# Counting three per cent more for a 512-column row in the planner's clock of a two-layer hybrid decoder trunk

## Chip, cores and metric

One core of one Trainium2 chip. The metric is the device time of one execution in microseconds; a kernel's time is the median of its runs. Beside the timed runs there is one profiled execution, from which every duration below is taken.

## What is computed

The reference is two layers of a decoder trunk on a sequence of 256 positions with 1024 features, in float32. Cut to what matters:

```
for i in range(2):
    h = rms_norm(x, norm_g[i])
    rq, rk, rv, rz, mq, mk, mv, mz = split(h @ w_in[i])        # 1024 -> 8 groups of 512
    r_out = silu(rz) * retention(rotary(rq), rotary(rk), rv, ret_norm_g[i])
    m_out = silu(mz) * moba(rms_norm(mq, q_norm_g[i]), rms_norm(mk, k_norm_g[i]), mv, rel_bias)
    x = x + concat([r_out, m_out]) @ w_out[i]                  # 1024 -> 1024
    gate = sigmoid(rms_norm(x) @ w_ple_gate[i])                # 1024 -> 1024
    x = x + gate * rms_norm(p[i] @ w_ple[i], ple_norm_g[i])    # 256 -> 1024
```

Retention has 4 heads of 128 with an exponential decay and a group norm per head. The block attention has 4 heads of 128; with 256 positions there is one block, so it is causal softmax attention with a relative bias.

## The kernel before

**Tiles.** The 256 positions are two row tiles (m = 0, 1) of 128. The 1024 features are 8 slices (k) of 128, so the activations lie transposed, as 128x128 stationary tiles. Weights are streamed as moving operands of 128x512. Each product of weights is made of three matmuls with split operands, high by high, high by low, low by high (`mm3`, L383, L384, L385); the parts are made by a copy on ScalarE (L336 for a weight, L635 for an activation) and a subtraction on VectorE (L339, L637). The first group of the first layer has its own routine (L531), and the per-layer embedding another (L720 to L722).

**Stages.** In each layer TensorE runs the eight input projections in the order MQ, MK, RQ, RK, MZ, MV, RV, RZ, then the output projection (first the slices k = 4 to 7, which are the attention's, then k = 0 to 3, the retention's), the embedding, and the gate projection. Each weight stage is 512 KB pieces of two slices: a load on SyncE's queue, a ScalarE copy, a VectorE subtraction. Results are turned back to transposed form by a ScalarE copy to 16-bit halves (L599), a DMA transpose on the same SyncE queue (L609) and VectorE copies (L618).

**Four groups of small matmuls** per layer are put in between the rows of the projections: `moba_scores` (L928, L910), `moba_out` (L938, which ends with the retention's own scores, L988), `ret_scores` (L910) and `ret_out` (L938). After `ret_out` comes a chain: statistics and scale of the group norm (L1009 to L1019), the normalising on ScalarE (L1026), the product with the gate RZ on VectorE (L1054, which reads the accumulator bank that RZ held, and L1059, after which the plan counts the bank as free), then turning, gain (L632) and split (L635, L637) into the stationary tiles that the output projection's slices k = 0 to 3 read. The accumulator pool `acc` has four banks, and RZ's two row tiles hold two of them while the output projection opens four accumulations.

**What sets the order.** The instruction streams of all engines are laid out at build time by the class `Flow`, a list scheduler written by hand. It keeps one clock per engine. Work that is not TensorE's is in chains (generators) whose steps have an engine and a cost in us; `pick` takes the step that can start first, and among those of one engine that can start the one with the smallest key. A chain's key is fixed when it begins (`flow.soon(slack)`: TensorE's clock then plus a slack), a weight stage's key is its due time less a lead of 5.7 to 9.6 us. TensorE's own order is the program's, and each step of it moves its clock: `flow.row(us)` first lays all other work that starts by then, and adds the us. The time that this clock shows is used in three ways:

```
ROW = 0.22
TILE = 12 * ROW
flow.row(3 * ROW * (1.0 if cols.stop - cols.start == GW else 0.53))      # in mm3, L381
return flow.clock[PE] + (i - now[0]) * TILE                               # due, L354
if any(c is None for c in cs) or not all(c.done and c.ready + margin <= flow.clock[PE] for c in cs):
    return                                                                # tick, L393
```

So ROW is the us that TensorE's clock counts for one matmul with 512 columns (L381, and L530 in the first group, L719 in the embedding), and twelve of them, TILE, are what one piece of weights is taken to last when due times are worked out. `tick` is asked after every second `mm3`, that is after six rows, and puts the next of the four groups in when all chains that it needs are finished and `margin` us have gone by on TensorE's clock (2.9, 2.0, 2.2 and 0.3 us). The small matmuls have costs of their own (0.22, 0.36), which are written as numbers, and so have all steps of the other engines. None of these numbers is an instruction: they decide only in which order each engine's instructions stand, and which of the borrowed buffers a weight piece gets. The engines then run by semaphores.

Of the kernel before, what the change touches and what calls it, by code (L numbers as in the profile page):

```python
# [50 lines left out]
EARLY = {0: FIRST, "late": S, ("K", 0): GW, 1: BLOCK, ("K", 1): GW, **{k: BLOCK for k in range(2, KT)}}  # L51

PE, ACT, DVE, POOL, SP = range(5)
ROW = 0.22
LANES, LINE = 4, 4
TILE = 12 * ROW
HOP = 0.15
# [186 lines left out]
def tile_hybrid_trunk(ctx: ExitStack, tc: tile.TileContext, early, x, pT, ple_g, rel_bias,  # L244
# [126 lines left out]
    def lanes(w):  # L371
        return w.rearrange("p (l t n) -> p t l n", t=LANES, n=LINE)

    def columns(w, sl):
        return lanes(w)[:, sl.start // P:sl.stop // P]

    def mm3(ps, a, m, k, stage, kk, start, stop, cols=slice(0, GW)):
        a.need(m, k)
        wh, wl = stage.part(kk // 2)[kk % 2]
        ah, al = a.of(m, k)  # L380
        flow.row(3 * ROW * (1.0 if cols.stop - cols.start == GW else 0.53))  # L381
        wh, wl = columns(wh, cols), columns(wl, cols)
# [129 lines left out]
    def first_rows(k, ps, start, stop, key=()):  # L512
# [9 lines left out]
        for i, (which, w, c) in enumerate(order):  # L522
# [3 lines left out]
            for j, sl in enumerate([slice(0, S), slice(S, GW)] if halves else [slice(0, GW)]):  # L526
                if j:
                    flow.need(firsts["late"])
                for m in range(MT):
                    flow.row(0.12 if halves else ROW)  # L530
                    nc.tensor.matmul(ps[m][:, sl], (a0.lo if which[0] == "lo" else a0.hi)[:, k, m * P:(m + 1) * P],  # L531
# [159 lines left out]
    def embed(l):  # L691
# [22 lines left out]
        for m in range(MT):  # L714
            ps = [bank(mix_p, "mix") for _ in range(2)]
            for n in range(2):
                for k, (wh, wl) in enumerate(w.part(n)):
                    ah, al = (v[:, k, m * P:(m + 1) * P] for v in (ph, pl))
                    flow.row(3 * ROW)  # L719
                    nc.tensor.matmul(ps[n], ah, lanes(wh), start=k == 0, stop=False)  # L720
# [564 lines left out]
```

## Time and profile before

| | |
|---|---|
| median of 3 runs | 300.57 us (299.64 to 301.93) |
| the profiled execution, device time | 301.4 us |
| its span, first to last instruction | 299.5 us |
| mean granted TensorE clock | 0.997 |
| VectorE, ScalarE, GpSimd busy | 254.7, 215.2, 31.5 us |
| DMA moved | 69.76 MB |

The profile counts busy time per engine: PE is TensorE's matmuls, PEld its loads of stationary tiles, DVE VectorE, ACT ScalarE, POOL GpSimd, SP SyncE with its DMA queue. A row of the timeline gives start, busy time, engine, line, operation and tiles, how many instructions it merges, and in brackets the idle time before it with what ended that. A row of the stages gives the stretch, its length, busy time with the number of instructions for each engine, the granted clock (PEclk), the DMA share and GB/s.

### The profile page before, as it was taken

The page shows a single profiled execution, that of the slowest core. Times are in us where ns is not written, and L with a number is a line of the kernel's source. Part 1 is how long each engine was busy: PE and PEld are TensorE (multiplying, and loading weights), DVE is VectorE, ACT ScalarE, POOL GpSimd, SP SyncE. Part 2 cuts the span into 40 slices and gives each one's busy share as a digit, 9 for nine tenths or more (in the row PEclk, how much of TensorE's full clock was granted, in tenths as well). Part 3 has the DMA queues.
Part 4 walks back from the last instruction along what each step waited for, and adds up shares of the span by engine and source line. Part 5 has one row for each costly group of instructions (what it writes and reads, how often), then busy time and mean ns, then how long its engine had stood idle before and what let it go on. Part 6 is the DMA issues. An engine that isn't in the chain of part 4 may idle for free.

```text
span 299.5 us, 4292 instructions
## 1 busy us (share of the span) xinstructions
PE 292.0 (98%) x1411; PEld 246.9 (82%) x1411; DVE 254.7 (85%) x461; ACT 215.2 (72%) x376; POOL 31.5 (11%) x44
## 2 busy tenths in 40 slices
PE   8999999999999989999999999999999999999994
PEld 4788888888899866888888888888889988888884
DVE  3968798999998999789999379999978899969932
ACT  3879966599755985998494696599764879499211
POOL 6005200000000300031003220000000030001200
PEclk9999999999999999999999999999999999999998
DMA  6999999999977858987789669857993994963011
GB/s 227 362 416 404 243 216 396 377 266 186 296 286 216 328 138 283 160 233 264 190 240 287 210 176 188 305 101 219 305 325 105 224 363 117 275 182 71 0 72 70
DMA packets 61773, 69.76 MB, mean 233 GB/s; under 512 B 46260, under 2 KB 47160, under 8 KB 61624
## 3 DMA queue, kind: packets, MB, share of 16 engines
q1 hardware_dynamic: 61712, 69.50, 77.8%
q8 instruction: 11, 0.18, 0.3%
q14 instruction: 10, 0.08, 0.1%
q0 software_dynamic: 32, 0.01, 0.0%
q10 hardware_dynamic: 8, 0.00, 0.0%
HBM read 57.42 MB, written 1.05 MB: 195 GB/s over the span
## 4 chain that ended last, share of the span: by engine, by line
PE 91%; DVE 3%; DMA 2%; ACT 1%; issue 1%; SPq 0%; DVEq 0%
PE acc L385 25%; PE acc L384 25%; PE acc L383 25%; PE acc L531 4%; PE mix L938 4%; PE mix L910 2%; DMA a<-in_early 2%; DVE wl L339 2%; PE mix L722 1%; PE mix L721 1%; PE mix L720 1%; PE mix L385 1%; PE mix L384 1%; PE mix L383 1%; PE mix L988 1%
## 5 line engine op out<-in xcount | busy, mean ns | idle before, releaser
L383 PE MATMUL acc<-wh,a 128*128 128x512 f32 (+1 forms) x292 | 110.3, 378 | 1.4 <-DVE tok L1054 1.4
L385 PE MATMUL acc<-wh,a 128*128 128x512 f32 (+1 forms) x292 | 109.9, 376 | 0.0
L384 PE MATMUL acc<-wl,a 128*128 128x512 f32 (+1 forms) x292 | 109.8, 376 | 0.0
L339 DVE TENSOR_TENSOR wl<-wst,wh 128x1024 fp32r<-128x1024 f32 x78 | 94.0, 1220 | 8.1 <-ACT wh L336 8.1
L336 ACT CAST wh<-wst 128x1024 fp32r<-128x1024 f32 x78 | 80.8, 1052 | 27.7 <-PE acc L385 18.0
L383 PEld LDWEIGHTS acc<-wh,a 128*128 128x128 f32 x292 | 54.8, 188 | 11.0 <-DVE tok L1054 1.8
L385 PEld LDWEIGHTS acc<-wh,a 128*128 128x128 f32 x292 | 54.8, 188 | 9.5
L384 PEld LDWEIGHTS acc<-wl,a 128*128 128x128 f32 x292 | 54.8, 188 | 9.2
L599 ACT COPY u<-tok 128x1024 uint16<-128x1024 uint16 x30 | 30.9, 1049 | 8.7 <-DVE tok L836 4.4
L651 POOL TENSOR_TENSOR ro<-rs_t,neghalf 128x4 f32<-128x4 f32 x4 | 5.8, 1460 | 133.2 <-DVE rs_t L649 133.2
L1160 ACT ACTIVATE tmp<-acc,hr 128x512 f32<-128x512 f32 (+1 forms) x9 | 5.8, 639 | 16.2 <-PE acc L385 16.2
L599 ACT COPY u<-x_t 128x1024 uint16<-128x1024 uint16 x12 | 12.5, 1042 | 6.3 <-DVE x_t L1116 5.1
L618 DVE COPY tmp<-w 128x512 uint16<-128x512 uint16 x40 | 15.9, 460 | 0.7 <-DMA w<-u 0.7
L635 ACT CAST a<-tmp 128x512 fp32r<-128x512 f32 x20 | 12.2, 617 | 5.7 <-DVE tmp L632 4.3
L637 DVE TENSOR_TENSOR a<-tmp,a 128x512 fp32r<-128x512 f32 x20 | 13.6, 686 | 0.5 <-ACT a L635 0.5
L618 DVE COPY T<-w 128x512 uint16<-128x512 uint16 x32 | 13.0, 464 | 1.0 <-DMA w<-u 0.9
L1163 DVE SCALAR_TENSOR_TENSOR tmp<-tmp,E 128x512 f32<-128x512 f32 (+1 forms) x9 | 5.7, 628 | 8.0 <-ACT tmp L1160 8.0
L938 PEld LDWEIGHTS mix<-V,PS 128*128 128x128 f32 x96 | 11.3, 192 | 0.3
L531 PE MATMUL acc<-wh,a 128*128 128x512 f32 (+1 forms) x42 | 11.0, 380 | 0.4 <-ACT wh L437 0.4
L938 PE MATMUL mix<-V,PS 128*128 128x128 f32 x96 | 11.4, 275 | 0.0
L383 PE MATMUL acc<-T,a 128*128 128x512 f32 x28 | 10.7, 383 | 0.0
L385 PE MATMUL acc<-T,a 128*128 128x512 f32 x28 | 10.7, 383 | 0.0
(143 smaller groups left out, 446.6 us busy)
## 6 DMA issues: line engine op xcount, KB each, us to landing
wst<-in_w_in SPq DMA_DIRECT2D x59, 512.0 KB, 6.1
wst<-in_w_out SPq DMA_DIRECT2D x16, 512.0 KB, 6.4
wst<-in_w_gate SPq DMA_DIRECT2D x16, 512.0 KB, 5.5
wst<-in_w_ple SPq DMA_DIRECT2D x4, 512.0 KB, 7.8
wst<-in_early SPq DMA_DIRECT2D x4, 384.0 KB, 7.1
a<-in_early SPq DMA_DIRECT2D x3, 384.0 KB, 5.8
x_t<-in_x SPq DMA_DIRECT2D x1, 1024.0 KB, 11.4
gb<-in_ple_g SPq DMA_DIRECT2D x2, 512.0 KB, 5.9
```

Of the source, the lines that this page charges most:

```text
L336: nc.scalar.copy(hi, s)
L339: nc.vector.tensor_tensor(lo, s, hi.bitcast(F32), op=ALU.subtract)
L383: nc.tensor.matmul(ps, ah, wh, start=start, stop=False)
L384: nc.tensor.matmul(ps, ah, wl, start=False, stop=False)
L385: nc.tensor.matmul(ps, al, wh, start=False, stop=stop)
L531: nc.tensor.matmul(ps[m][:, sl], (a0.lo if which[0] == "lo" else a0.hi)[:, k, m * P:(m + 1) * P], columns(w, sl), start=start and i + j == ...
L599: nc.scalar.copy(u, src.bitcast(U16).rearrange("p (n t) -> p t n", t=2))
L618: nc.vector.tensor_copy(v, w[:, t].rearrange("p (h b) k -> p h (b k)", h=v.shape[1]))
L635: nc.scalar.copy(h, src)
L637: nc.vector.tensor_tensor(a.lo[:, k0:k0 + 4, m * P:(m + 1) * P], src, h.bitcast(F32), op=ALU.subtract)
L910: nc.tensor.matmul(ps, w[a], x[b], start=i == 0, stop=i == 2)
L938: nc.tensor.matmul(ps[:, h * DH:(h + 1) * DH], lhs(h, m, b), v[:, b, h * DH:(h + 1) * DH], start=b == 0, stop=b == m)
```

## The change

One constant: the clock counts 0.227 us for a row in place of 0.22, and TILE with it 2.724 us in place of 2.64. No instruction is added or taken away, and no size, buffer or slack is changed.

```
-ROW = 0.22
+ROW = 0.227
 LANES, LINE = 4, 4
 TILE = 12 * ROW
```

## Prediction

> **What bounds the kernel now.** I read the page first, then TensorE's waits, then stages, then the timeline where TensorE waits. The page's engine totals:
>
> ```profile
> span 299.5 us, 4292 instructions
> PE 292.0 (98%) x1411; PEld 246.9 (82%) x1411; DVE 254.7 (85%) x461; ACT 215.2 (72%) x376; POOL 31.5 (11%) x44
> ```
>
> TensorE is busy almost throughout, VectorE is next. The list of TensorE's own waits:
>
> ```profile
> PE acc L383 <- DVE tok L1054: 1.4, 1, 1.4
> PE mix L282 <- PEq L1274: 0.8, 1, 0.8
> PE acc L531 <- ACT wh L437: 0.4, 1, 0.4
> PE acc L385 <- DVE a L637: 0.4, 1, 0.4
> PE acc L383 <- ACT a L635: 0.2, 1, 0.2
> ```
>
> The second and third are the start. The other three are one place, found by cutting the span into stages of TensorE alone (start:end, length, busy and instructions, clock, DMA share, GB/s):
>
> ```profile
> 8.64:50.58 41.94, 41.94 (x190) 1.00 0.99 335
> 50.58:84.59 34.01, 34.01 (x165) 1.00 1.06 295
> 105.68:116.44 10.76, 8.80 (x37) 1.00 0.75 212
> 116.44:191.48 75.04, 75.04 (x338) 1.00 0.82 227
> 294.80:299.50 4.70, 0.39 (x4) 0.79 0.14 49
> ```
>
> The first row has 190 matmuls back to back, 41.94 / 190 = 0.2207 us each. The fourth has 338, two of them running in from before: 75.04 / 336 = 0.2233 us. So the planner's old 0.22 was 0.3% short in one stretch and 1.5% in the other, and the new 0.227 is 2.9% and 1.7% long. The chip's rows do not move with the constant, only the order does. In the third stage 12 triples start, 36 x 0.2233 = 8.04 us of work in 10.76 us: **2.72 us are lost**, and that is all that order can still give in the middle. The last stage, 4.70 us, is the tail after the last matmul.
>
> **The place of the loss** is the first layer's output projection. TensorE there:
>
> ```profile
> 92.28 2.84 PE L938 MATMUL mix<-V,PS 128*128 128x128 f32 x24
> ...
> 100.32 0.38 PE L383 MATMUL acc<-wh,a 128*128 128x512 f32 x1
> ...
> 106.13 0.38 PE L385 MATMUL acc<-wh,a 128*128 128x512 f32 x1
> 107.92 0.49 PE L383 MATMUL acc<-wh,a 128*128 128x512 f32 x1 [1.41 <-DVE tok L1054]
> ...
> 114.11 0.48 PE L385 MATMUL acc<-V,a 128*128 128x512 f32 x1 [0.38 <-DVE a L637]
> ```
>
> and VectorE, which it waits for:
>
> ```profile
> 103.58 0.69 DVE L1054 TENSOR_TENSOR tok<-T,acc 128x512 f32<-128x512 f32 x1 [0.30 <-ACT T L1026]
> 104.30 0.69 DVE L1059 SCALAR_TENSOR_TENSOR tok<-tmp,tok 128x512 f32<-128x512 f32 x1
> 104.91 2.35 DVE L339 TENSOR_TENSOR wl<-wst,wh 128x1024 fp32r<-128x1024 f32 x2
> 107.18 0.68 DVE L1054 TENSOR_TENSOR tok<-T,acc 128x512 f32<-128x512 f32 x1
> 107.90 0.69 DVE L1059 SCALAR_TENSOR_TENSOR tok<-tmp,tok 128x512 f32<-128x512 f32 x1
> 108.51 2.35 DVE L339 TENSOR_TENSOR wl<-wst,wh 128x1024 fp32r<-128x1024 f32 x2
> ...
> 113.37 0.68 DVE L637 TENSOR_TENSOR a<-tmp,a 128x512 fp32r<-128x512 f32 x1
> ```
>
> ret_out starts at 92.28. The matmul at 107.92 would open the fourth accumulation, but its bank is RZ's second row tile's, held until L1054 has read it at 107.86. TensorE could have been there at 106.13 + 0.22 = 106.35, 14.07 us after ret_out; the bank came 15.6 us after it. Next, the retention's stationary tile is done at 114.05, 21.8 us after ret_out; without any wait its low part would be wanted at 100.32 + 16 triples of 0.67 + 0.45 = 111.49. The difference, 2.6 us, is the loss again. The second layer has the same chain and no wait:
>
> ```profile
> 235.82 2.84 PE L938 MATMUL mix<-V,PS 128*128 128x128 f32 x24
> ...
> 252.57 0.39 PE L383 MATMUL acc<-T,a 128*128 128x512 f32 x1
> ...
> 257.71 0.38 PE L385 MATMUL acc<-K,a 128*128 128x512 f32 x1
> ```
>
> ```profile
> 250.75 0.69 DVE L1054 TENSOR_TENSOR tok<-T,acc 128x512 f32<-128x512 f32 x1 [0.49 <-ACT T L1026]
> ...
> 255.80 0.69 DVE L637 TENSOR_TENSOR a<-tmp,a 128x512 fp32r<-128x512 f32 x1
> ```
>
> The bank is free 251.44 - 235.82 = 15.6 us after ret_out, as in the first layer, and the tile done after 20.7 us. But TensorE arrives 16.75 us after ret_out, for here 12 triples of RZ follow ret_out, where the first layer has 8. The loss is thus a matter of **where ret_out stands among the rows**: it is some two ticks too late, each tick being six rows, 6 x 0.2233 = 1.34 us.
>
> **The change, part by part.** It removes and adds nothing, so 292.0 us of matmuls stay. It moves three things.
>
> (1) The groups. Between 8.64 and 84.59 stand some 335 rows: 190 of the first stage, and of the second's 165 all but the 20 small ones of moba_scores. TensorE's planned clock is 335 x 0.007 = 2.35 us later at the same row. Whether a group comes forward depends on what its gate hangs on. If it is a chain that TensorE started a few rows before, the gate moves with the clock and nothing changes; if it is VectorE's backlog, which the plan counts in unchanged us, the group comes forward by 2.35 / 1.32 = 1.8 ticks. moba_out's gate is the latter, by VectorE's load (stage columns: PE, PEld, DVE, ACT, POOL) and its last input:
>
> ```profile
> 45.00:84.00 39.00, 39.00 (x189) 33.59 (x188) 37.17 (x55) 29.95 (x47) 0.00 (x0) 1.00 1.06 306
> ```
>
> ```profile
> 82.95 0.80 DVE L618 COPY T<-w 128x512 uint16<-128x512 uint16 x2
> ```
>
> VectorE is busy 37.17 of 39 us, and the last turned piece of RK is written until 83.75, 0.84 us ahead of moba_out at 84.59. Counting only from moba_scores, with 145 rows, the shift is 1.0 us or 0.8 tick. Between 0 and 2 ticks I take one, the nearest to both counts. ret_scores and ret_out follow it, as they wait for its banks and for V, which it frees. One tick forward takes 1.34 us off the 2.72.
>
> (2) Due times. A piece that is n pieces ahead is due 0.084 n us later, so weights give way a little more to chains: for a step ready at the same moment the chain goes first. Fillers such as the two L339 at 104.91 were laid because nothing else was ready, so most stay. I cost it at nothing, because no PE wait in the list is for L336 or L339 after the start; without that cover one misplaced L339 costs 2.35 / 2 = 1.17 us.
>
> (3) All other order, on ACT, DVE and SyncE's queue (weight loads, transposes and the constants' loads stand in one line there). What hides it is the lead of the stationary tiles, thinnest for the next layer's fifth slice and for the second layer's L637 above (257.71 - 256.49 = 1.22 us):
>
> ```profile
> 160.53 0.68 DVE L637 TENSOR_TENSOR a<-tmp,a 128x512 fp32r<-128x512 f32 x1
> ```
>
> ```profile
> 162.45 0.39 PE L385 MATMUL acc<-V,a 128*128 128x512 f32 x1
> ```
>
> Here it is 162.45 - 161.21 = 1.24 us. One extra L339 ahead of either (1.17 us) is just covered, two would cost 1.1 us. I take 0.2 us in all, nearer the covered end, since either needs two.
>
> Sum: 301.4 (profiled time, its span of 299.5 and 1.9 around it) - 1.34 + 0.2 = 300.26. The median of runs is 0.83 under the profiled execution, so **299.4 us** on its scale. The bounds: below, -2.72, 297.85; above, two extra L339 in the old place (2.34) and in both thin ones (2 x 1.1), +4.5, 305.1.
>
> The Trainium skill ("Perfetto Trace Analysis", Identifying the Most-Contended Engine) holds matmul occupancy a bad measure of headroom and LDWEIGHTS occupancy a good one. By it the 82% above would leave a sixth of the span. The trace does not agree for this question: 336 matmuls of this shape follow each other at 0.2233 us without a gap, so reordering has 2.72 us to give.
>
> **Rivals.** B, no shift where it counts: the gate moves with TensorE's clock, or the tick (asked only every six rows) rounds the shift away; the constant then does not do what it says. For it: 0.8 of a tick is under one. Against: both counts are well over half. Time 300.6.
>
> C, slower. One mechanism: the planned TensorE is now slower than the real one everywhere, so in the saturated stretch from ret_out to the output projection the plan sees 72 rows x 0.0037 = 0.27 us of room that is not there, and non-urgent splits are laid into the retention's chain. Two more L339 ahead of L1054 and L637, with ret_out where it was, make the loss 2.72 + 2.34 = 5.06: time 302.9. It decides once more than one L339 enters and no tick is gained. For it: four L339 already stand between the chain's steps in the rows above. Against: the second layer runs the same chain in 20.7 us with just such fillers.
>
> C', the same with the clock lost. The stage row at 105.68 shows clock 1.00 although TensorE stood still up to 1.41 us at a time; the tail row shows 0.79 after the last matmul. So the clock goes down when TensorE stands still for longer, and the tail prices one such episode at 4.70 x 0.21 = 1.0 us; on C that makes 303.9. The Trainium skill ("TensorE: Matmul & The Clock Gate", What's actually happening) gives half rate after an idle window of some 3.4 us; the trace agrees so far, with full clock through 1.41 us. If some 3.4 us of rows then ran at half rate, an estimate from that page, C would come to 304.6.
>
> D, two ticks: the loss is gone, as in the second layer: 300.57 - 2.72 = 297.85, with 0.2 of new waits 298.1.
>
> **How the numbers follow.** Forecast 0.42, B 0.20, C 0.18, C' and worse 0.06, D 0.14. The range takes in D and C, and leaves out C' and what lies under D: 297.7 to 303.5. A measurement tells about 1% from no change, 3 us here: faster means under 297.56, slower over 303.58. D passes the first for a quarter of its chance, as runs spread by 0.9 us: 0.04. Slower has C', a third of C, and 0.02 of causes not named: 0.14. The rest, 0.82, is within 1%.
>
> **What would show it.** Right: no instruction more or less on any engine; ret_out of the first layer at about 91 us, 10 triples of RZ behind it in place of 8; TensorE's wait for L1054 about 0.1 to 0.3 us, with the loss near 1.4 us; the pitch of rows still 0.2207 and 0.2233. Wrong: ret_out at 92.3 still (B); L1054's wait longer, with L339 ahead of it, or new PE waits for L637 at the gate projection or the second layer's start (C); the output projection without any wait (D).

## The result, and the profile after

The changed kernel takes 299.15 us (median of 18 runs, 297.32 to 301.29), the kernel before 300.97 us in the same series (299.55 to 303.35). The ratio is 0.9938, 95% interval 0.9919 to 0.9957: 1.9 us less, with 1.3 to 2.4 in the interval. The forecast was a gain of 1.1 us, to 299.4 us. The profiled execution took 297.32 us, with a span of 295.4 us. Its engine totals, and TensorE's waits:

```profile
span 295.4 us, 4301 instructions
PE 290.3 (98%) x1411; PEld 247.6 (84%) x1411; DVE 254.0 (86%) x461; ACT 214.6 (73%) x376; POOL 34.1 (12%) x44
```

```profile
PE mix L282 <- PEq L1274: 0.8, 1, 0.8
PE acc L383 <- DVE tok L1054: 0.2, 1, 0.2
```

The numbers of instructions on the five engines are the same as before, and of the three waits at the first layer's output projection one is left, at 0.2 us in place of 1.4. Two stages tell where the time went: the whole output projection with the embedding up to the gate projection, and a stretch of 55 us behind it (TensorE alone; start:end, length, busy and instructions, clock, DMA share, GB/s). Before:

```profile
100.32:129.84 29.52, 27.56 (x121) 1.00 0.79 212
130.00:185.00 55.00, 55.00 (x248) 1.00 0.78 223
```

After:

```profile
99.84:126.91 27.07, 26.84 (x121) 1.00 0.72 209
130.00:185.00 55.00, 55.00 (x252) 1.00 0.86 253
242.70:269.50 26.80, 26.80 (x121) 1.00 0.59 165
```

The first stage holds 120 matmuls of 512 columns; at 0.2233 us without a wait they are 26.80 us, which is just what the second layer takes for them. So 2.72 us were lost before, and now the stage is 0.27 us longer than those 26.80. The waiting itself still costs about 0.5 us: from 111.73 us on the rows follow each other at 0.2200 us, 69 of them in 15.18 us where 0.2233 would make 15.41, and this hides 0.23 us of it. So order took 2.2 us off the loss.

The second row was not foreseen: in the same 55 us, with no gap, four matmuls more begin. The rows are at 0.2200 us there too, which makes 66.61 - 65.69 = 0.92 us from the first layer's gate projection to the second layer's MZ. The rest of the two spans' difference of 4.1 us, some 0.7, lies mostly ahead of the second group and in the tail; the second group begins at 18.28 us here, at 18.89 before, and at 18.64 in another profile of the changed kernel.

The place that was read before, TensorE and then VectorE:

```profile
89.11 2.84 PE L938 MATMUL mix<-V,PS 128*128 128x128 f32 x24
...
106.26 0.49 PE L383 MATMUL acc<-T,a 128*128 128x512 f32 x1 [0.23 <-DVE tok L1054]
```

```profile
102.67 2.36 DVE L339 TENSOR_TENSOR wl<-wst,wh 128x1024 fp32r<-128x1024 f32 x2
105.51 0.69 DVE L1054 TENSOR_TENSOR tok<-T,acc 128x512 f32<-128x512 f32 x1 [0.48 <-ACT T L1026]
106.24 0.69 DVE L1059 SCALAR_TENSOR_TENSOR tok<-tmp,tok 128x512 f32<-128x512 f32 x1
106.85 1.22 DVE L339 TENSOR_TENSOR wl<-wst,wh 128x1024 fp32r<-128x1024 f32 x1
...
110.56 0.69 DVE L637 TENSOR_TENSOR a<-tmp,a 128x512 fp32r<-128x512 f32 x1
```

ret_out stands two ticks earlier, 12 triples ahead of the output projection in place of 8, as the second layer always had it. TensorE could have been at the fourth bank 16.75 us after ret_out. But the chain did not keep its length: the bank came at 106.20, 17.1 us after ret_out, where it took 15.6 us before.

### The profile page after: what moved, and what is told of

It is laid out like the page before. It is cut to its first block, busy times and chain, and to the rows that moved or that the text cites. A ratio compares the mean times of both kernels' runs of the same rounds, so it can differ in the third digit from the quotient of the medians.

```text
span 295.4 us, 4301 instructions
## 1 busy us (share of the span) xinstructions
PE 290.3 (98%) x1411; PEld 247.6 (84%) x1411; DVE 254.0 (86%) x461; ACT 214.6 (73%) x376; POOL 34.1 (12%) x44
## 4 chain that ended last, share of the span: by engine, by line
PE 73%; DVE 13%; DMA 7%; issue 4%; ACT 3%; DVEq 0%; ACTq 0%
PE acc L383 20%; PE acc L384 19%; PE acc L385 19%; DVE wl L339 5%; PE acc L531 5%; DMA w<-u 4%; DMA wst<-in_w_ple 3%; DVE T L618 2%; PE mix L938 2%; PE mix L282 1%; PE mix L721 1%; PE mix L720 1%; PE mix L722 1%; PE mix L910 1%; ACT wh L336 1%
## 5 line engine op out<-in xcount | busy, mean ns | idle before, releaser
L383 PE MATMUL acc<-wh,a 128*128 128x512 f32 (+1 forms) x286 | 108.1, 378 | 0.0
L385 PE MATMUL acc<-wh,a 128*128 128x512 f32 (+1 forms) x286 | 107.8, 377 | 0.0
L384 PE MATMUL acc<-wl,a 128*128 128x512 f32 (+1 forms) x286 | 107.7, 377 | 0.0
L339 DVE TENSOR_TENSOR wl<-wst,wh 128x1024 fp32r<-128x1024 f32 x76 | 92.0, 1220 | 7.7 <-ACT wh L336 7.4
L336 ACT CAST wh<-wst 128x1024 fp32r<-128x1024 f32 x76 | 78.4, 1053 | 12.3 <-PE acc L385 4.6
L385 PEld LDWEIGHTS acc<-wh,a 128*128 128x128 f32 x286 | 53.6, 188 | 9.1
L383 PEld LDWEIGHTS acc<-wh,a 128*128 128x128 f32 x286 | 53.7, 188 | 8.9
L384 PEld LDWEIGHTS acc<-wl,a 128*128 128x128 f32 x286 | 53.7, 188 | 8.9
L599 ACT COPY u<-tok 128x1024 uint16<-128x1024 uint16 x30 | 31.0, 1051 | 14.4 <-DVE tok L956 9.2
L599 ACT COPY u<-x_t 128x1024 uint16<-128x1024 uint16 x12 | 12.5, 1042 | 10.0 <-DVE x_t L1116 6.5
L637 DVE TENSOR_TENSOR a<-tmp,a 128x512 fp32r<-128x512 f32 x20 | 13.7, 685 | 0.0
L811 POOL TENSOR_TENSOR qr<-qms,neghalf 128x4 f32<-128x4 f32 x8 | 10.5, 1317 | 11.0 <-DVE qms L809 11.0
L938 PEld LDWEIGHTS mix<-V,PS 128*128 128x128 f32 x96 | 11.3, 192 | 0.3
L383 PE MATMUL acc<-T,a 128*128 128x512 f32 (+1 forms) x30 | 11.1, 371 | 0.2 <-DVE tok L1054 0.2
L938 PE MATMUL mix<-V,PS 128*128 128x128 f32 x96 | 11.4, 275 | 0.0
L531 PE MATMUL acc<-wh,a 128*128 128x512 f32 (+1 forms) x42 | 11.1, 382 | 0.0
```

Of the source, the lines that this page charges most:

```text
L336: nc.scalar.copy(hi, s)
L339: nc.vector.tensor_tensor(lo, s, hi.bitcast(F32), op=ALU.subtract)
L383: nc.tensor.matmul(ps, ah, wh, start=start, stop=False)
L384: nc.tensor.matmul(ps, ah, wl, start=False, stop=False)
L385: nc.tensor.matmul(ps, al, wh, start=False, stop=stop)
L599: nc.scalar.copy(u, src.bitcast(U16).rearrange("p (n t) -> p t n", t=2))
```

## The experiments

The place theory says that the gain is ret_out of the first layer standing earlier among the rows. Its rivals say that it is the length of the counted row, or the later due times with what they do to VectorE's order. All ratios are to the kernel before on the same chip. The places of a layer's four groups are given as the count of `mm3` triples ahead of them: before 48, 96, 98, 100 and 232, 280, 282, 288; after 44, 88, 90, 96 and 232, 274, 276, 288.

**Due times alone.**

```
-TILE = 12 * ROW
+TILE = 12 * 0.227
```

> Only the due times count 0.227 (TILE = 12 * 0.227), the clock's rows stay at 0.22. The place theory (the gain is ret_out of the first layer standing earlier among the rows) looks at where the groups land: here ret_out stands 12 triples ahead of the output projection, as in the changed kernel, so 299.0 to 299.8 us, ratio near 0.995, TensorE's wait for L1054 under 0.5 us. The rival, the clock theory (the gain needs the rows counted longer), expects 300.5 to 301.3 and a loss of some 2.7 us at the output projection.

Measured: 299.63 us, ratio 0.9974 (0.9954 to 0.9994). ret_out did move by two ticks (92, 94, 96); TensorE waits 0.5 us for L637, none for L1054, and the stage of 120 matmuls takes 27.53 us. So due times by themselves bring the groups forward, presumably because steps of the chains are then chosen ahead of weights and the gates open sooner.

**The clock alone.**

```
-ROW = 0.22
-TILE = 12 * ROW
+ROW = 0.227
+TILE = 12 * 0.22
```

> Only the clock's rows count 0.227, due times stay at 12 * 0.22. All groups land where the changed kernel has them. Place theory and clock theory: 298.7 to 299.6 us, ratio near 0.994, wait for L1054 0 to 0.5 us. A third theory, that weights giving way to chains by their later due times makes the gain, expects 300.5 to 301.3 here.

Measured: 298.88 us, 0.9957 (0.9935 to 0.9979), all places as in the changed kernel, the stage 27.27 us. Either half of the constant is enough to bring ret_out two ticks forward.

**The places alone, and the places undone.** `tick` is made to go by a list instead of the clock, in the kernel before with the places of after, and the other way round. Cut to the two tests that change:

```
-            if any(c is None for c in cs) or not all(c.done and c.ready + margin <= flow.clock[PE] for c in cs):
+            if rows3[0] < AT[0]:
                 return
-            if sum(t + (0 if conds else margin) <= flow.clock[PE] for t in flow.free_at["mix"]) < banks:
+            if [flow.force() for c in cs for _ in iter(lambda: c.done, True)] and not AT:
```

The margin and the test for free banks fall away, and `flow.force()` first lays whatever steps the group still needs. So no run moves a place alone: the work that follows a group, and what is laid beside it, move along.

> The kernel before with 0.22 everywhere, but the four groups of each layer are put in after as many triples as in the changed kernel. Place theory: 298.7 to 299.8 us, the loss at the output projection under 1 us. Clock theory and due-time theory (the order of VectorE's and ScalarE's work makes the gain, and the places go along with it): 300.3 to 301.5.

> The changed kernel with 0.227 everywhere, but the groups put back to where the kernel before has them. Place theory: 300.5 to 301.5 us, the loss at the output projection back at 2 to 3 us with TensorE waiting for L1054. Clock and due-time theories: 298.8 to 299.8.

Measured: places only 298.94 us, 0.9944 (0.9922 to 0.9965); places undone 302.27 us, 1.0062 (1.0037 to 1.0087). The stage in the first:

```profile
101.79:128.59 26.80, 26.80 (x122) 1.00 0.72 196
```

Nothing is lost, with 0.22 everywhere. In the second the stage is shown for both layers, and TensorE's waits:

```profile
99.83:128.90 29.07, 27.41 (x121) 1.00 0.73 207
245.43:273.43 28.00, 27.06 (x122) 1.00 0.64 168
```

```profile
PE acc L385 <- DVE a L637: 1.3, 2, 0.9
PE acc L383 <- ACT a L635: 1.3, 1, 1.3
```

The loss is back in the first layer, 29.07 - 26.80 = 2.27 us, and a new one of 1.20 us stands in the second, where the kernel before had none. This settles it between the theories: the places, with the order that follows from them, make the gain. Two things went past the expectation. TensorE does not wait for L1054, whose bank is free 14.1 us after ret_out, but for the tile, which is done after 21.4 us. And with the old places the longer count is not neutral but worse than 0.22, by 0.6%. In the second layer the cause can be read: four L339 stand between the second L1054 and the tile's L637 where the kernel before has two, and the tile is done 22.9 us after ret_out in place of 20.7.

The times of these four runs do not add up with their stages. Against the kernel before the stages give 2.0, 2.25 and 2.72 us less and, with the places undone, 0.75 us more; the ratios give 0.8, 1.3 and 1.7 us less and 1.9 us more. All four are 1.0 to 1.2 us worse than their stages. No profile of the kernel before was taken beside these runs, where its median is 300.35 us (300.57 to 301.47 in the other series), so what makes the difference stays open. With the places undone part of it may be lost clock: four of the twelve runs show a mean granted clock of 0.994, and took 302.0 to 304.2 us.

**The size of a tick.** The list with the first layer's last three groups one tick (94, 96, 98) and two ticks (92, 94, 96) earlier.

```
-    groups, AT = [], [48, 96, 98, 100, 232, 280, 282, 288]
+    groups, AT = [], [48, 94, 96, 98, 232, 280, 282, 288]
```

> The kernel before, 0.22 everywhere, with the last three groups of the first layer one tick earlier: moba_out after 94 triples, ret_scores after 96, ret_out after 98 in place of 100; the second layer as before. Place theory, by the arithmetic of the prediction (1.34 us a tick): the loss at the output projection falls from 2.7 to about 1.4 us, 299.0 to 299.7 us. Rival, that the whole set of groups in both layers matters: 300.2 to 301.0.

> As the last, two ticks earlier: 92, 94 and 96 triples, first layer alone. Place theory: loss 0 to 0.6 us, 298.3 to 299.2 us, as good as the kernel with all places of the changed one (298.94). Rival, that moba_scores and the second layer's groups have a share: 299.5 to 301.

Measured: one tick 299.02 us, 0.9916 (0.9891 to 0.9940); two ticks 298.99 us, 0.9915 (0.9883 to 0.9947). One tick already takes the whole loss at the output projection. Its stage, and its VectorE:

```profile
100.53:127.33 26.80, 26.80 (x122) 1.00 0.78 212
```

```profile
101.37 0.68 DVE L1054 TENSOR_TENSOR tok<-T,acc 128x512 f32<-128x512 f32 x1
...
105.37 0.69 DVE L1054 TENSOR_TENSOR tok<-T,acc 128x512 f32<-128x512 f32 x1
...
110.42 0.68 DVE L637 TENSOR_TENSOR a<-tmp,a 128x512 fp32r<-128x512 f32 x1
```

ret_out starts at 91.14 here. The bank comes 14.9 us after it and the tile 20.0 us, where before it was 15.6 and 21.8: the chain itself became shorter. Of the 1.8 us, 1.1 lie ahead of the first L1054 (10.2 us after ret_out here, 11.3 before); the rest lies behind it, where five L339 stood up to the tile's L637 before, and four do now. With two ticks the tile is late again, 22.6 us after ret_out, and TensorE waits 0.5 us for it; the stage takes 27.58 us. So the expected 1.4 us for one tick was wrong; how many fillers fall into the chain changes with every shift.

**Shorter and longer counts.**

```
-ROW = 0.22
+ROW = 0.2207      (the other: 0.234)
```

> ROW = 0.2207, what a row took in the first stretch of the profile before, a third of one per cent over 0.22. The plan already puts the first layer's last three groups one tick earlier with it (ret_out after 98 triples). Place theory: the loss is gone, 298.5 to 299.5 us, ratio 0.991 to 0.996, as with one tick alone; what counts is not that the clock runs long. Rival, that three per cent of length is what gains: 300.3 to 301.3.

> ROW = 0.234, six per cent more. ret_out stands after 96 triples as in the changed kernel, moba_out still earlier. Place theory alone: 298.5 to 299.5 us. If a clock that counts too long also lays fillers into chains, as with the places undone, the leads of the stationary tiles (0.5 to 1.5 us at the gate projection and the second layer's start with 0.227, 2 to 4 us with 0.22) are used up and TensorE waits for L635 or L637: 300 to 303 us.

> The changed kernel once more, on the chip of these runs: ratio 0.992 to 0.996. Its profile tells whether the return of the rows to 0.2200 us at 111.5 us belongs to the kernel (then 0.2200 from 112 to 187 us again) or to that execution (then 0.2233 there, as in the other profiles).

Measured: 0.2207 gives 305.32 us, ratio 1.0132 (1.0089 to 1.0175); 0.234 gives 303.29 us, 1.0070 (1.0044 to 1.0096); the changed kernel again 299.28 us, 0.9928 (0.9898 to 0.9958). With 0.2207 the expectation failed: ret_out stands after 98 triples, as with one tick, yet the kernel is 1.3% slower. TensorE in its output projection, and VectorE ahead of it:

```profile
113.38 0.49 PE L383 MATMUL acc<-K,a 128*128 128x512 f32 x1 [1.88 <-ACT a L635]
113.70 0.39 PE L384 MATMUL acc<-K,a 128*128 128x512 f32 x1
115.89 0.79 PE L385 MATMUL acc<-K,a 128*128 128x512 f32 x1 [1.80 <-DVE a L637]
116.48 0.63 PE L383 MATMUL acc<-K,a 128*128 128x512 f32 x1
```

```profile
103.43 0.68 DVE L1054 TENSOR_TENSOR tok<-T,acc 128x512 f32<-128x512 f32 x1
...
106.62 2.35 DVE L339 TENSOR_TENSOR wl<-wst,wh 128x1024 fp32r<-128x1024 f32 x2
108.89 1.22 DVE L339 TENSOR_TENSOR G<-wst,T 128x1024 fp32r<-128x1024 f32 x1
110.02 1.22 DVE L339 TENSOR_TENSOR wl<-wst,wh 128x1024 fp32r<-128x1024 f32 x1
...
114.02 1.22 DVE L339 TENSOR_TENSOR T<-wst,T 128x1024 fp32r<-128x1024 f32 x1
115.15 1.29 DVE L637 TENSOR_TENSOR a<-tmp,a 128x512 fp32r<-128x512 f32 x2
```

ScalarE in the same stretch:

```profile
105.09 1.09 ACT L336 CAST wh<-wst 128x1024 fp32r<-128x1024 f32 x1
106.03 1.10 ACT L599 COPY u<-tok 128x1024 uint16<-128x1024 uint16 x1
```

The banks come in time here; it is the tile that is late, 24.6 us after ret_out. Its L1054, the first of the two, starts at 103.43, two us later than with one tick. ScalarE then begins its turning copy (L599) only at 106.03, behind a weight copy (L336) among others, 1.2 us after L1059 ended at 104.84; with one tick it followed after 0.1 us. Four L339 fill VectorE while the transposed halves are on their way; these landed at 110.24, so only the last of the four is in the way. At the end the second row tile's steps and a fifth L339 stand ahead of L637, so that both row tiles' L637 end up together. TensorE loses 1.9 us, runs two matmuls, loses 1.8 us more, and then something else is lost as well:

```profile
113.30:116.50 3.20, 1.32 (x4) 0.75 1.00 376
116.50:121.80 5.30, 5.30 (x14) 0.51 0.48 195
```

The granted clock is 0.51 over these 5.30 us; it had gone down at 114.9 us, 0.8 us into the second wait, and was back at 121.7. Rows follow each other there at 0.43 us, 116.48 to 116.91 to 117.34 in the timeline, and the twelve of them cost some 2.5 us. The stage takes 33.83 us, a loss of 7.03. With 0.234 moba_out comes after 84 triples, ret_out stands where the changed kernel has it, and TensorE waits in several places behind the start:

```profile
PE acc L384 <- DVE wl L339: 0.7, 1, 0.7
PE acc L385 <- DVE a L637: 0.7, 1, 0.7
PE acc L383 <- DVE G L856: 0.7, 1, 0.7
PE mix L910 <- DVE tok L956: 0.3, 1, 0.3
PE mix L938 <- ACT V L846: 0.2, 1, 0.2
```

Among them is a weight (L339), which no other profile of these has behind its start. They come to 2.6 us, against 2.0 in the kernel before, so they account for only part of the 2.1 us that this kernel is slower. The place theory alone does not cover either kernel: the place decides when the chain may start, but what the plan lays into the chain on VectorE and ScalarE is worth as much.

**The pitch of the rows.** One matmul of 256 columns more behind ret_out in each layer, whose outcome nobody reads: in the kernel before, and in the one with the places alone; then twelve of them in the kernel with one tick.

```
+            one = mix_p.tile([P, GW], F32, name="mix")
+            nc.tensor.matmul(one[:, :S], aT.hi[:, 0, :P], aT.hi[:, 0], start=True, stop=True)
             flow.free("PS", flow.clock[PE])
```

> The kernel before with one matmul more behind ret_out in each layer, 128x256, into a free bank that nobody reads; its outcome is not used, so the output is the same. In the profiles the rows of 512 columns follow each other at 0.2233 us after ret_out until the next group of 256-column matmuls (L910), and at 0.2200 behind it. If such a matmul itself brings the quicker pitch back: rows at 0.2200 from 95 to 190 us and from 238 to 290 us, some 2.0 us less work, less 0.2 us for the two matmuls: 298.6 to 299.2 us. If it is a wait or something else that does: no change, 300.4 to 301.

> The kernel with 0.22 and the places of the changed one (298.94 us), with the same one matmul more behind ret_out in each layer. If the matmul brings the quicker pitch back: 297.0 to 297.8 us. If not: 298.9 to 299.3.

> The kernel with one tick, and behind ret_out in each layer twelve 128x256 matmuls as L910 has them, into a bank that nobody reads; the output is the same. They take 1.4 us a layer, so no gain is looked for. If a run of such matmuls brings the quicker pitch: rows at 0.2200 us behind them until the next layer's groups. If what L910 reads or where it stands does it: 0.2233 as before.

Measured: 301.68 us, 1.0009 (0.9991 to 1.0028) on the kernel before; 299.17 us, 0.9924 (0.9898 to 0.9949) on the places; 300.8 us in one run with twelve. The stretch from 130 to 185 us in these three:

```profile
130.00:185.00 55.00, 55.00 (x248) 1.00 0.78 224
```

```profile
130.00:185.00 55.00, 55.00 (x248) 1.00 0.81 240
```

```profile
130.00:185.00 55.00, 55.00 (x251) 1.00 0.87 243
```

Such a matmul does not bring the quicker pitch back. In the kernel before with one matmul more it was there for a while behind the wait of 1.4 us, from 108.05 to 112.23 us, and gone again after the next two waits. With twelve it came back, but only at 137 us, long behind them. The changed kernel's second profile has 252 matmuls in that stretch again, so there the return belongs to the kernel; the kernels without added matmuls have 247 to 249 otherwise. What does it stays open.

## Why the prediction was right, step by step

- **The bound and the place of the loss** held. 2.72 us is what order can give: the best kernels here, one and two ticks, gain 0.85%, 2.5 us; the one with one tick loses nothing in that stage, the other 0.8 us.
- **The groups come forward** held in kind. In size it was two ticks for ret_out where one was taken, and four for moba_out. The counts were low: moba_scores came forward by two ticks itself (48 to 44 triples) with the clock alone, and the later due times alone move moba_out by two. That VectorE's backlog holds its gate was argued and is not shown. That ret_out follows moba_out was half right: 8 triples lie between them now, 4 before.
- **A tick is worth 1.34 us** failed. It held the chain behind ret_out for fixed at 15.6 and 21.8 us. The runs show 14.1 to 17.1 us for the bank and 20.0 to 24.6 for the tile, and one tick worth 2.72. The two errors went against each other: two ticks with the bank 1.5 us later in the chain leave about 0.5 us lost, where one tick with the old chain would have left 1.4. In the profiled pair order thus gave 2.2 us, twice the 1.14 of the sum; that the time came out so near to the forecast is in part luck. Of the signs that the prediction gave, two ticks are those of rival D, and the wait that is left is that of the forecast.
- **Due times cost nothing** failed in its reason: they alone move ret_out by two ticks. As they push the same way as the clock, the sum did not show it.
- **Other order at 0.2 us** held for waits, none is new. But its cover was spent: the low part of the second row tile's first slices for the next layer's projections is done 0.5 us before it is wanted (153.28 against the third matmul at 153.75), where the kernel before had 3.4 us:

```profile
152.59 0.69 DVE L637 TENSOR_TENSOR a<-tmp,a 128x512 fp32r<-128x512 f32 x1
```

```profile
153.75 0.38 PE L385 MATMUL acc<-T,a 128*128 128x512 f32 x1
```

- **Rival C** is a mechanism that exists: with the places undone two L339 more stand in the second layer's chain and TensorE loses 1.2 us there, and with 0.234 the waits spread. In the changed kernel the chain is longer too, 22.1 us to the tile, but with two ticks at 0.22 it is 22.6 us; so there the longer count is not shown to be the cause. **Rival C'** exists as well, in the kernel with 0.2207, and the rows at the lower clock cost some 2.5 us, where the tail had priced 1.0. It was expected after one longer standstill; the clock fell within the second of two waits, when TensorE had stood still for 1.9 and 0.8 us with two matmuls between. The Trainium skill ("TensorE: Matmul & The Clock Gate", What's actually happening) puts it at an idle window of some 3.4 us. Here the clock fell some 3.4 us after the first wait began, at 111.50, but the stretch was not idle throughout; the half rate agrees with the 0.51.
- **Not foreseen**: the return of the quicker pitch, 0.92 us in the profiled pair and 0.23 us more in the output projection. How much of the median's 1.9 us it makes is not settled, for the pitch of the first stretch (0.2207 in the profile before) is 0.2233 in part of the other profiles, whatever the kernel.

## What to carry to other kernels

When a hand-written planner's clock is changed, count how many slots each block of the bottleneck engine moves, and read from the trace which wait that slot feeds; the constant's closeness to the chip says little (0.2207 was just what a row took in the first stretch of the profile before, and gave the slowest kernel). Then fix the block's place by itself and leave the constant: one tick by a list did no worse than the constant did. Do not price a shift with the chain behind it held fixed, since each shift lays other fillers into the chain, and one filler more or less (1.17 us) is nearly as much as the slot (1.34 us).

## What the runs showed of the hardware

- Rows of 512 columns have two steady pitches at full granted clock, 0.2200 and 0.2233 us, 1.5% apart. In every profile the rows behind ret_out (128-column matmuls on unsplit operands, L938) have the slower one, and those behind the second layer's scores (L910) the quicker one again. In the changed kernel it came back in between, at 111.7 and at 112.7 us in its two profiles, in the kernel with twelve matmuls more at 137 us, and in the kernel before with one matmul more for 4 us behind a wait.
- In the kernel with 0.2207 the granted clock was down to half from 114.9 to 121.7 us. It fell within the second of two waits, of 1.9 and 1.8 us with two matmuls between, while a single wait of 1.41 us in the kernel before left it at 1.00. In the tails of the fourteen profiles it fell between 2.2 and 4.9 us after the end of the last matmul, so the runs show no single length of standing still that decides.
